# Sums of weight blocks in two channel mixers: by adding DMA transfers instead of adds on VectorE and GpSimd

## The chip, the cores and the metric

The kernel runs on one core of a Trainium2 chip. The metric is the device time of one execution in microseconds (us), from three timed executions of the kernel before. The trace that is read below is one further, profiled execution.

## The reference

The program is a two-layer backbone over 512 latent and 256 context tokens of width 1024: attention, then a SwiGLU channel mixer, in both layers. The change touches only the input projection of the channel mixers. What they compute, in float32:

```python
D_MODEL = 1024
D_FF = -(-8 * D_MODEL // (3 * 256)) * 256      # 2816

def swiglu(h, w_in, w_out):
    g, u = jnp.split(h @ w_in, 2, axis=-1)
    return (jax.nn.silu(g) * u) @ w_out

# per layer l; the context stream is updated only in layer 0
x = x + g_f * swiglu(modulate(rms_norm(x, norm_ffn_g[l]), sh_f, sc_f), ffn_w_in[l], ffn_w_out[l])
```

## The kernel before

**Precision.** TensorE multiplies a 32-bit format of lower precision, so each matrix is split into a high part (a cast on ACT, line 193) and a low part (the matrix less its high part, on VectorE or GpSimd, line 195), and each product is three matmuls (`mm3`, lines 206 to 208): high by high, high by low, low by high. `split_w` makes the pair `wh`, `wl` of a weight tile.

**One block of the mixer.** The 2816 gate columns and the 2816 up columns are taken in `FT` = 22 blocks of 128. Block j of `w_in` is a 2 by 2 matrix of tiles: A11 and A12 are the gate columns by the lower and the upper half of the model dimension, A21 and A22 the up columns. The tokens are two halves too (384 tokens each in layer 0, 256 each in layer 1), so B is also 2 by 2. Instead of eight products of tiles, the kernel makes seven (Winograd's form of Strassen's scheme), from these sums of weights: S1 = A21 + A22, S2 = S1 - A11, S3 = A11 - A21, S4 = A12 - S2. The sums of B (T1 to T4) are made once per mixer in `wino_h`. Each tile of A is 128 partitions by 512 float32, 256 KB.

**Where the weights are made.** `forms` is a generator of seven steps for one block, one per product: 11, 12, S2, S3, S1, 22, S4. Step 1 loads A11 and A12 through SyncE's queue (`load_raw`, line 184) and splits A11; step 2 splits A12; step 3 loads A21 and A22, makes S3 (line 1141), S1 (line 1142, in place of A21) and S2 (line 1143, in place of A11), and splits S2; steps 4 to 6 split S3, S1 and A22; step 7 makes S4 (line 1152, in place of A12) and splits it. `FA_ADD` and `F_ADD` say which engine adds: in layer 0 GpSimd (p) makes all four, in layer 1 VectorE (v) makes S3 and S1 and GpSimd makes S2 and S4.

**Order of the work.** `stream` strings the steps of all blocks together: two steps of blocks 0 and 1, then their five others, then all seven of each further block. `up` consumes products, and before each one `use` draws steps from the stream until 5 (layer 0) or 6 (layer 1) more are made than used. The first five steps are drawn earlier, during the second half of the attention's output projection (`ahead`). `up` then combines the seven products of a block on VectorE (lines 1198 to 1229) into gate and up tiles, and `out` multiplies them and splits the result (lines 1193 to 1196; GpSimd in layer 0, VectorE in layer 1). `down` multiplies finished blocks by the output weights in chunks of three or four blocks, interleaved with the products of the next chunk. In layer 0, VectorE also computes the next layer's modulation vectors beside the mixer (`mod_mac`, lines 392 and 394), from weights that are loaded into the same ring of buffers.

**Buffers.** Raw weights of every kind in the mixer share one ring of 10 tiles in layer 0 and 8 in layer 1 (tag `wr`); the pairs `wh`, `wl` have 5 and 6; S3 has 2 tiles of its own (tag `ws`, `NWS`). Each engine and each DMA queue works in order, and a tile framework puts in the waits. The order on each engine comes from its scheduler.

Of the kernel before, what the change touches and what calls it, by code (L numbers as in the profile page):

```python
# [10 lines left out]
F32 = mybir.dt.float32  # L11
# [3 lines left out]
ALU = mybir.AluOpType  # L15
# [3 lines left out]
P = 128  # L19
# [7 lines left out]
SPREAD0, SPREAD1 = 3, 4  # L27
AHEAD = 2
STATS_AT = 1
FA_ADD = ("pppp", "vvpp")  # L30
F_ADD = ("pppp", "vvpp")
F_LO = ("vvvvvvv", "vvvvvvv")
MACS = (0, 4, 5, 1, 6, 7, 2, 8, 9, 3, 10, 11)
MAC_LAG = 3
# [10 lines left out]
NWS = 2  # L45
# [51 lines left out]
def f32(ap):  # L97
    return ap.bitcast(F32)


class Kernel:
# [1022 lines left out]
    def forms(self, layer, j, f):  # L1124


        fa, lo = (F_ADD if j >= AHEAD else FA_ADD)[layer], F_LO[layer]

        def raw(i, h):
            return self.load_raw(self.I["w_in"][layer, j, i][:, h:h + 512], 512)  # L1130

        def split(i, name, a):
            f[name] = self.split_w(a, 512, lo_by=lo[i])
        a11, a12 = raw(0, 0), raw(0, 512)
        split(0, "11", a11)
        yield
        split(1, "12", a12)
        yield
        a21, a22 = raw(1, 0), raw(1, 512)
        s3 = self.wp.tile([P, 512], F32, tag="ws", name=self.nm("ws"), bufs=NWS)  # L1140
        self.by(fa[0]).tensor_sub(s3, a11, a21)
        self.by(fa[1]).tensor_add(a21, a21, a22)
        self.by(fa[2]).tensor_sub(a11, a21, a11)  # L1143
        split(2, "S2", a11)
        yield
        split(3, "S3", s3)
        yield
        split(4, "S1", a21)
        yield
        split(5, "22", a22)  # L1150
        yield
        self.by(fa[3]).tensor_sub(a12, a12, a11)
        split(6, "S4", a12)
        yield

# [15 lines left out]
    def up(self, layer, j, B, n, z, stream, together):  # L1171


        nc = self.nc
        v = nc.vector
        f = self.f[j]

        def use(count=1):
            self.used += count
            while self.ready < self.used + LOOK[layer]:  # L1180
                if next(stream, 0) == 0:
                    break

        def prod(a, b):
            use()
            ps = self.psM()[:, :n]
            for k in range(4):
                ws = slice(k * P, (k + 1) * P)
                self.mm3(ps, (f[a][0][:, ws], f[a][1][:, ws]), B[b][k], k == 0, k == 3)
            return ps  # L1190

        def out(g, u, half):
            self.by(Z_MUL[layer][half]).tensor_mul(g, g, u)
            zh, zl = (t[:, half * n:half * n + n] for t in z[j])
            nc.scalar.copy(zh, g)
            self.by(Z_LO[layer][half]).tensor_sub(zl, g, f32(zh))
        p, c11 = self.c_tile(n), self.c_tile(n)
        nc.scalar.copy(p, prod("11", "11"))
        yield
        v.tensor_add(c11, p, prod("12", "21"))  # L1200
        yield
        five = (("S2", "T2"), ("S3", "T3"), ("S1", "T1"), ("22", "T4"), ("S4", "22"))
        if together:

            use(5)
            ps = [self.psM()[:, :n] for _ in five]
            for k in range(4):
                ws = slice(k * P, (k + 1) * P)
                for i in (4, 2, 1, 0, 3):
                    x, y = five[i]  # L1210
                    self.mm3(ps[i], (f[x][0][:, ws], f[x][1][:, ws]), B[y][k], k == 0, k == 3)
            ps = iter(ps)
        else:
            ps = (prod(*x) for x in five)
        v.tensor_add(p, p, next(ps))
        nc.scalar.activation(c11, c11, AF.Silu)
        yield
        u3, c22 = self.c_tile(n), self.c_tile(n)
        v.tensor_add(u3, p, next(ps))
        yield  # L1220
        q = next(ps)
        v.tensor_add(c22, u3, q)
        v.tensor_add(p, p, q)
        yield
        v.tensor_add(u3, u3, next(ps))
        z[j] = self.new_z()
        out(c11, u3, 0)
        yield
        v.tensor_add(p, p, next(ps))
        self.last_silu = nc.scalar.activation(p, p, AF.Silu)  # L1230
        out(p, c22, 1)
        yield
# [709 lines left out]
```

## Time and profile before

| | us |
|---|---|
| three timed runs | 1801.03, 1806.44, 1806.47 |
| their median | 1806.44 |
| the profiled execution | 1802.62 |
| its span, first to last instruction | 1800.8 |

| engine | busy us | share of the span |
|---|---|---|
| TensorE matmul (PE) | 1698.3 | 94% |
| VectorE (DVE) | 1425.6 | 79% |
| ACT | 926.0 | 51% |
| GpSimd (POOL) | 509.0 | 28% |

In the span, layer 0's mixer is prepared from about 440 us and runs to about 1050 us; layer 1's is prepared from about 1405 us and runs to the end. TensorE's mean granted clock is 0.974 of full speed. The DMA queues moved 186.21 MB, 103 GB/s over the span, of which GpSimd's software queue moved 8.49 MB, all of it outside the mixers. Matmuls overlap, so the duration of one is longer than the time between two.

### The profile page before, as it was taken

How to read it: one execution, taken by the hardware profiler on the slowest of the kernel's cores; microseconds unless marked ns; L12 is line 12 of the kernel's file. 1: busy time of each engine (PE TensorE's matmuls, PEld its weight loads, DVE VectorE, ACT ScalarE, POOL GpSimd, SP SyncE). 2: the span in 40 equal slices, each digit the busy share in tenths (PEclk: the TensorE clock that was granted, in tenths of full speed). 3: DMA queues.
4: the chain of work that ended last, by engine and by line, in shares of the span. 5: the costliest groups of instructions: out<-in, count | busy, mean ns of one | idle time of the engine just before them, and what ended most of it. 6: DMA issues, size and time to landing. Idle time of an engine off the chain costs nothing. (4 is left out here: it accounts for less than half of the span.)

```text
span 1800.8 us, 30907 instructions
## 1 busy us (share of the span) xinstructions
PE 1698.3 (94%) x11032; PEld 1592.9 (88%) x11032; DVE 1425.6 (79%) x3060; ACT 926.0 (51%) x2222; POOL 509.0 (28%) x586
## 2 busy tenths in 40 slices
PE   6899999999898999999999989999999879999999
PEld 5789888999778999999989988999998869999997
DVE  4788877566788888888888677888788689888886
ACT  5566668655553333333323466776676555444442
POOL 1400002211674443444443252222221342111110
PEclk9999999999889999999999999999999989999999
DMA  9533233234113434344334313111123423333332
GB/s 315 172 113 116 81 99 99 62 115 158 33 41 108 130 111 133 110 122 128 104 111 141 97 44 105 48 53 48 48 71 110 139 63 106 106 106 100 106 100 83
DMA packets 125754, 186.21 MB, mean 103 GB/s; under 512 B 10625, under 2 KB 63504, under 8 KB 125600
## 3 DMA queue, kind: packets, MB, share of 16 engines
q1 hardware_dynamic: 119360, 172.53, 31.1%
q0 software_dynamic: 2496, 8.49, 1.5%
q10 hardware_dynamic: 3744, 3.23, 0.6%
q8 instruction: 87, 1.43, 0.3%
q14 instruction: 67, 0.55, 0.1%
HBM read 174.70 MB, written 13.70 MB: 105 GB/s over the span
## 5 line engine op out<-in xcount | busy, mean ns | idle before, releaser
L193 ACT CAST wh<-wr 128x512 fp32r<-128x512 f32 (+4 forms) x465 | 287.7, 624 | 385.8 <-PE psM L207 232.3
L195 DVE TENSOR_TENSOR wl<-wr,wh 128x512 fp32r<-128x512 f32 (+3 forms) x433 | 353.2, 819 | 49.0 <-ACT wh L193 42.9
L208 PE MATMUL psD<-zh,wl 128*128 128x384 f32 (+1 forms) x512 | 185.4, 362 | 16.7 <-DVE wl L195 16.7
L206 PE MATMUL psD<-zh,wh 128*128 128x384 f32 (+1 forms) x512 | 184.0, 359 | 6.4 <-ACT wh L193 6.4
L711 PE MATMUL psW<-wh,hh 128*128 128x384 f32 (+2 forms) x543 | 183.4, 339 | 3.9 <-ACT wh L193 3.2
L207 PE MATMUL psD<-zl,wh 128*128 128x384 f32 (+1 forms) x512 | 183.4, 358 | 0.0
L712 PE MATMUL psW<-wl,hh 128*128 128x384 f32 (+2 forms) x543 | 181.2, 334 | 0.0
L713 PE MATMUL psW<-wh,hl 128*128 128x384 f32 (+2 forms) x543 | 179.8, 332 | 0.0
L207 PE MATMUL psM<-bl,wh 128*128 128x256 f32 x616 | 174.8, 284 | 3.9 <-POOL bl L467 3.6
L206 PE MATMUL psM<-bh,wh 128*128 128x256 f32 x616 | 173.8, 284 | 4.8 <-ACT bh L466 2.7
L208 PE MATMUL psM<-bh,wl 128*128 128x256 f32 x616 | 172.7, 281 | 0.0
L207 PE MATMUL psM<-hl,wh 128*128 128x384 f32 (+1 forms) x416 | 139.4, 335 | 3.2 <-POOL hl L467 2.8
L206 PE MATMUL psM<-hh,wh 128*128 128x384 f32 (+1 forms) x416 | 139.8, 337 | 2.6 <-ACT hh L466 1.8
L195 POOL TENSOR_TENSOR wl<-wr,wh 128x512 fp32r<-128x512 f32 (+2 forms) x32 | 39.8, 1248 | 352.4 <-ACT wh L193 330.4
L1143 POOL TENSOR_TENSOR wr<-wr,wr 128x512 f32<-128x512 f32 x44 | 60.8, 1383 | 273.9 <-DVE wl L195 225.4
L208 PE MATMUL psM<-hh,wl 128*128 128x384 f32 (+1 forms) x416 | 137.9, 331 | 0.0
L394 DVE SCALAR_TENSOR_TENSOR wr<-wr,silc,wr 128x512 f32<-128x512 f32 x112 | 105.4, 950 | 27.1 <-DMA wr<-in_mod_w 26.7
L207 PEld LDWEIGHTS psM<-bl,wh 128*128 128x128 f32 x616 | 118.1, 192 | 8.5 <-POOL bl L467 6.1
L206 PEld LDWEIGHTS psM<-bh,wh 128*128 128x128 f32 x616 | 117.7, 192 | 8.1 <-ACT bh L466 3.8
L208 PEld LDWEIGHTS psD<-zh,wl 128*128 128x128 f32 x512 | 96.8, 189 | 30.8 <-DVE wl L195 23.3
L1371 POOL TENSOR_TENSOR nbm<-nb,namask 128x128 f32<-128x128 f32 x144 | 64.7, 466 | 200.4 <-DVE nam L1399 180.0
L208 PEld LDWEIGHTS psM<-bh,wl 128*128 128x128 f32 x616 | 117.9, 191 | 0.0
(414 smaller groups left out, 4789.4 us busy)
## 6 DMA issues: line engine op xcount, KB each, us to landing
wr<-in_w_in SPq DMA_DIRECT2D x176, 256.0 KB, 2.9
wr<-in_mod_w SPq DMA_DIRECT2D x96, 256.0 KB, 2.7
mraw<-in_mod_w SPq DMA_DIRECT2D x32, 512.0 KB, 4.0
wr<-in_w_dn SPq DMA_DIRECT2D x50, 256.0 KB, 2.7
wr<-in_w_na SPq DMA_DIRECT2D x28, 384.0 KB, 3.2
wr<-in_w_out SPq DMA_DIRECT2D x36, 256.0 KB, 2.7
wr<-in_w_dn SPq DMA_DIRECT2D x48, 192.0 KB, 2.4
modw<-in_mod_w SPq DMA_DIRECT2D x8, 1024.0 KB, 9.6
```

The source lines that it names most:

```text
L193: nc.scalar.copy(hi[:, :n], raw[:, :n])
L195: (nc.gpsimd if on_pool else nc.vector).tensor_sub(lo[:, :n], raw[:, :n], f32(hi[:, :n]))
L206: t.matmul(out, w[0], x[0], start=first, stop=False)
L207: t.matmul(out, w[0], x[1], start=False, stop=False)
L208: t.matmul(out, w[1], x[0], start=False, stop=last)
L394: v.scalar_tensor_tensor(acc[cd], raw, self.sc[:, k, cd:cd + 1], acc[cd], ALU.mult, ALU.add)
L711: nc.tensor.matmul(ps, hh[:, ts], hi[:, o:o + n], start=k == 0, stop=False)
L712: nc.tensor.matmul(ps, hh[:, ts], lo[:, o:o + n], start=False, stop=False)
L713: nc.tensor.matmul(ps, hl[:, ts], hi[:, o:o + n], start=False, stop=k == KD - 1)
L1143: self.by(fa[2]).tensor_sub(a11, a21, a11)
L1371: nc.gpsimd.tensor_tensor(o, bj[:, t0 + t], m, ALU.add)
```

## The change

All four sums of a block are made by DMA transfers that add what they read to what stands at their destination (`accum_op=ALU.add`), issued from GpSimd's queue. Such a transfer can only add, so the signs are turned: the block is treated as if A11 and A12 were negated. With S1 = A21 + A22 as before, S2 = A11 + S1, S3' = A11 + A21 and S4' = A12 + S2. The products of 11, S3' and S4' then come with the other sign, and three combinations on VectorE in `up` become subtractions of the same shape.

A21 gets A22 added straight from device memory; a second copy of A11 is loaded into S3's tile, and A21 is added to it from device memory; the finished S1 tile is added to A11's tile, and the finished S2 tile to A12's tile, both from one place in SBUF to another. The loads of A21 and A22 move from step 3 to step 2, ahead of the split of A12. The four adds on VectorE or GpSimd of each block go. Per block that is one more plain load of 256 KB on SyncE's queue and four adding transfers of 256 KB on GpSimd's; there are 44 blocks in the two layers.

```diff
-FA_ADD = ("pppp", "vvpp")
-F_ADD = ("pppp", "vvpp")
@@ forms
-        fa, lo = (F_ADD if j >= AHEAD else FA_ADD)[layer], F_LO[layer]
+        lo = F_LO[layer]
+
+        def src(i, h):
+            return self.I["w_in"][layer, j, i][:, h:h + 512]
 
         def raw(i, h):
-            return self.load_raw(self.I["w_in"][layer, j, i][:, h:h + 512], 512)
+            return self.load_raw(src(i, h), 512)
+
+        def add(t, x):
+            self.nc.gpsimd.dma_start(t, x, accum_op=ALU.add)
 
         def split(i, name, a):
             f[name] = self.split_w(a, 512, lo_by=lo[i])
-        a11, a12 = raw(0, 0), raw(0, 512)
+        a11, a12 = (t[:, :512] for t in (raw(0, 0), raw(0, 512)))
         split(0, "11", a11)
         yield
+        a21, a22 = (t[:, :512] for t in (raw(1, 0), raw(1, 512)))
+        s3 = self.wp.tile([P, 512], F32, tag="ws", name=self.nm("ws"), bufs=NWS)
+        nc = self.nc
+        nc.sync.dma_start(s3, src(0, 0))
+        add(a21, src(1, 512))
+        add(s3, src(1, 0))
         split(1, "12", a12)
         yield
-        a21, a22 = raw(1, 0), raw(1, 512)
-        s3 = self.wp.tile([P, 512], F32, tag="ws", name=self.nm("ws"), bufs=NWS)
-        self.by(fa[0]).tensor_sub(s3, a11, a21)
-        self.by(fa[1]).tensor_add(a21, a21, a22)
-        self.by(fa[2]).tensor_sub(a11, a21, a11)
+        add(a11, a21)
         split(2, "S2", a11)
         yield
         split(3, "S3", s3)
         yield
+        add(a12, a11)
         split(4, "S1", a21)
         yield
         split(5, "22", a22)
         yield
-        self.by(fa[3]).tensor_sub(a12, a12, a11)
         split(6, "S4", a12)
         yield
@@ up
-        v.tensor_add(p, p, next(ps))
+        v.tensor_sub(p, next(ps), p)
...
-        v.tensor_add(u3, p, next(ps))
+        v.tensor_sub(u3, p, next(ps))
...
-        v.tensor_add(p, p, next(ps))
+        v.tensor_sub(p, next(ps), p)
```

## Rows read from the trace of the kernel before

**Rows 1.** Stretches: start:end us, length, busy us (x instructions), clock, DMA share, GB/s.
```profile
440.00:520.00 80.00, 67.11 (x289) 57.15 (x288) 64.33 (x117) 46.28 (x103) 51.38 (x41) 0.81 0.19 64
600.00:700.00 100.00, 95.70 (x549) 94.21 (x548) 86.98 (x146) 32.65 (x62) 42.10 (x34) 1.00 0.38 117
...
1415.00:1420.00 5.00, 2.12 (x14) 1.83 (x12) 1.64 (x5) 3.11 (x7) 0.00 (x0) 0.81 0.81 302
1440.00:1470.00 30.00, 19.98 (x102) 15.85 (x102) 25.55 (x48) 18.37 (x43) 16.63 (x19) 0.84 0.15 48
1600.00:1700.00 100.00, 100.00 (x710) 92.80 (x708) 87.00 (x160) 49.13 (x93) 15.53 (x12) 1.00 0.35 104
```

**Rows 2.** Waits of TensorE, 440 to 1050 us: total us, times, longest us.
```profile
PE psD L208 <- DVE wl L195: 15.1, 10, 3.9
PE psD L206 <- ACT wh L193: 6.4, 1, 6.4
...
PE psM L208 <- POOL wl L195: 2.6, 1, 2.6
```

**Rows 3.** Timeline of VectorE in layer 1's mixer: start us, us, engine line operation.
```profile
1606.11 0.68 DVE L195 TENSOR_TENSOR wl<-wr,wh 128x512 fp32r<-128x512 f32 x1
...
1611.64 1.21 DVE L195 TENSOR_TENSOR wl<-wr,wh 128x512 fp32r<-128x512 f32 x1 [0.17 <-ACT wh L193]
```

**Rows 4.** Groups of VectorE, 565 to 1045 us: busy us, mean ns | idle before.
```profile
L195 DVE TENSOR_TENSOR wl<-wr,wh 128x512 fp32r<-128x512 f32 x116 | 96.2, 830 | 11.6 <-ACT wh L193 11.3
L394 DVE SCALAR_TENSOR_TENSOR wr<-wr,silc,wr 128x512 f32<-128x512 f32 x100 | 91.8, 926 | 27.1 <-DMA wr<-in_mod_w 26.7
```

**Rows 5.** Groups of GpSimd, 565 to 1045 us: the four adds.
```profile
L1143 POOL TENSOR_TENSOR wr<-wr,wr 128x512 f32<-128x512 f32 x18 | 26.0, 1447 | 39.3 <-DVE wl L195 24.6 <-DMA wr<-in_mod_w 10.1 <-issue 4.3
L1141 POOL TENSOR_TENSOR ws<-wr,wr 128x512 f32<-128x512 f32 x17 | 24.2, 1426 | 91.7 <-DMA wr<-in_w_in 87.0 <-DVE wl L195 4.7
L1142 POOL TENSOR_TENSOR wr<-wr,wr 128x512 f32<-128x512 f32 x17 | 23.8, 1398 | 9.0 <-DMA wr<-in_w_in 5.8 <-DVE x L1098 1.3 <-DVE wl L195 1.2
L1152 POOL TENSOR_TENSOR wr<-wr,wr 128x512 f32<-128x512 f32 x18 | 23.6, 1311 | 47.8 <-DVE wl L195 32.6 <-issue 12.6 <-DMA wr<-in_mod_w 2.7
```

**Rows 6.** Groups of the whole span by shape: VectorE's adds in layer 1.
```profile
L1141 DVE TENSOR_TENSOR ws<-wr,wr 128x512 f32<-128x512 f32 x22 | 17.0, 773 | 1.5 <-DMA wr<-in_w_in 1.4
...
L1142 DVE TENSOR_TENSOR wr<-wr,wr 128x512 f32<-128x512 f32 x22 | 15.1, 684 | 0.7 <-DMA wr<-in_w_in 0.6
```

**Rows 7.** GpSimd's DMA issues in the attention of layer 1: ns min/median/max.
```profile
L1364 POOL DMA_DIRECT2D nb<-rpb_exp x16: 546/563/622, 1070.3 to 1327.7; - x16
```

**Rows 8.** The page's DMA issues: count, KB each, median us to landing.
```profile
mraw<-in_mod_w SPq DMA_DIRECT2D x32, 512.0 KB, 4.0
...
nb<-rpb_exp POOLq DMA_DIRECT2D x16, 256.0 KB, 2.9
```

**Rows 9.** The 176 loads of mixer weights, 256 KB each: time to landing.
```profile
DMA to landing us min/median/max: 2.4/2.9/7.2
```

**Rows 10.** Timeline of GpSimd in layer 1's mixer: S2's adds of two blocks.
```profile
1611.01 1.29 POOL L1143 TENSOR_TENSOR wr<-wr,wr 128x512 f32<-128x512 f32 x1 [12.02 <-DVE wl L195]
...
1626.31 1.30 POOL L1143 TENSOR_TENSOR wr<-wr,wr 128x512 f32<-128x512 f32 x1 [12.04 <-DVE wl L195]
```

**Rows 11.** Timeline of ACT in layer 1's mixer: casts after that of A12.
```profile
1613.66 0.62 ACT L193 CAST wh<-wr 128x512 fp32r<-128x512 f32 x1 [2.05 <-PE psD L207]
...
1616.46 0.62 ACT L193 CAST wh<-wr 128x512 fp32r<-128x512 f32 x1 [0.69 <-PE psM L207]
```

**Rows 12.** Waits of ACT, 1515 to 1740 us: total us, times, longest.
```profile
ACT wh L193 <- PE psM L207: 58.2, 83, 0.9
```

**Rows 13.** The chain that ended last, in order of time: start us, us, what.
```profile
1409.37 6.75 DMA wr<-in_w_in
...
1506.20 1.63 POOL wr L1143
```

**Rows 14.** Waits of VectorE, 600 to 1000 us: total us, times, longest.
```profile
DVE wr L394 <- DMA wr<-in_mod_w: 25.5, 30, 1.6
```

## Prediction

> **What bounds the kernel now.** I read the page first (TensorE busy for 94% of the span), then the table of stretches, then the waits of TensorE inside the mixers, then the timelines of the engines that feed it, and last the chain that ended last. The table shows two kinds of stretch [rows 1]. Inside the mixers TensorE is the bound: 95.70 of 100 us in layer 0 and 100.00 of 100 us in layer 1, at full clock. On the way into a mixer it is not: 67.11 of 80 us from 440 us on, at a clock of 0.81, and 19.98 of 30 us from 1440 us on, at 0.84. So in the steady part of layer 1 nothing that feeds TensorE can gain; the gain can only come from layer 0's steady part and from the two ways in. What TensorE waits for in layer 0 is the low parts of weights from VectorE, 15.1 us in ten waits, one wait of 6.4 us for a cast, and one of 2.6 us for a low part that GpSimd makes, which stands behind adds on GpSimd's queue [rows 2]. VectorE is busy for 87 of 100 us in both layers [rows 1], so small delays on it reach TensorE.
>
> **What the change removes.** In layer 0, four adds per block on GpSimd, 1447 + 1426 + 1398 + 1311 ns = 5.6 us per block, 97.6 us between 565 and 1045 us [rows 5]. GpSimd has slack, so its own time is worth nothing but for the queue. What they cost is VectorE's time: the same subtraction of 128 by 512 takes 0.68 us when GpSimd rests and 1.21 us while GpSimd makes S2 and S4 [rows 3, 10]. In layer 0 the mean is 830 ns over 116 [rows 4], so 116 x 0.15 = 17 us are such waiting; at the same 18% another 17 us of L394's 91.8. The adds are 97.6 of 480 us, 20 in 100, against GpSimd's 42.10 in 100 altogether [rows 1], so about half of those 34 us goes, 17 us of VectorE in 480.
>
> The Trainium skill (SBUF — State Buffer, Who interferes with whom) says that a VectorE instruction with two SBUF inputs contends with a GpSimd instruction that reads SBUF, by a lock that is held for the whole instruction. The trace's 0.68 against 1.21 us agrees.
>
> In layer 1, two adds per block on VectorE, 773 + 684 ns, together 32.1 us [rows 6], and two on GpSimd. TensorE waits for neither in the steady part, so they are worth nothing there.
>
> **What it adds.** Per block four issues on GpSimd, by the only issues there that the trace has at 0.563 us each [rows 7], so 2.3 us, against 5.6 us of adds before; it is less than before even at twice that. One more load on SyncE, hidden as long as the ring has room.
>
> The unknown is L, the time from the issue of an adding transfer of 256 KB to its landing; the trace has none. From below: 2.9 us, a plain transfer of that size from the same queue [rows 8]. From above: 7.2 us, the slowest load of that size among loads that queue behind each other [rows 9]. An adding transfer reads both addends, 512 KB, and a plain load of 512 KB takes 4.0 us [rows 8]. I take 4 us, and keep both ends.
>
> The Trainium skill (Collectives: The Full Stack, The bandwidth ceiling) says that an adding transfer costs twice a copy because it issues two reads, and that the addition itself costs nothing. No row here shows it; by it L would be near my 4 us.
>
> **Where that time lies.** In layer 1 a block takes 1626.31 - 1611.01 = 15.3 us [rows 10]. The add into A11 may start when the low part of A11 is done, at 1611.0, and the cast of S2 is one of those at 1613.66 to 1616.46 [rows 10, 11]: 2.7 to 5.5 us for L. If L is longer, ACT waits for the rest, and behind it in its order the casts of S3, S1 and of the output weights. But casts run ahead: ACT waits for TensorE to free `wh`, 83 times [rows 12], and with six pairs and some ten casts in 15.3 us the lead is 6 x 1.53 = 9 us, less 1.3 us for cast (0.62) and low part (0.68): 7 to 8 us [rows 3, 11]. So S2 reaches TensorE late only if L is above 10 us or so.
>
> The tighter loop is GpSimd's own queue. The add into A11 waits for the sum in A21 to land, the add into A12 waits for the sum in A11 to land, and the next block's first add stands behind it: two landings and two issues that are not covered, 2 L + 1.1 us plus some hand-over, about 2 L + 2 per block. At L = 4 that is 10 of 15.3 us; it binds from L = 6.6 on. Queued behind a waiting issue in layer 0 are the multiplications of gate and up tiles, and behind those ACT's casts of them; the adds of before stood there too and waited for the same low parts, so at L = 4 the extra is some 3 us per block, and finished blocks are needed a chunk later.
>
> **The transfers.** In layer 1 the engines are busy for 0.35 at 104 GB/s [rows 1], so full is 297 GB/s, 4.5 MB in 15.3 us, of which 1.6 are used. Added are 0.26 MB for the load and 4 x 0.52 MB if both reads count: 3.9 MB, 87%. If the writes count as much, 5.0 MB, 110%. Layer 0 has a like share (0.38) and longer blocks.
>
> **The ways in.** At layer 1's, the chain that ended last runs for 6.75 us through a load of mixer weights, while the transfers move 302 GB/s at 0.81 [rows 1, 13]: every transfer that now stands ahead costs 0.87 us (262 KB at 302 GB/s). Block 1's A11 and A12 now queue behind block 0's A21, A22 and S3, 2.6 us, and share with up to four adding transfers, 4 x 1.7 = 7 us more. What ACT does behind those casts (the squares of the norm) is on the chain. Ends 0 and +9.5 us for each way in; I take +1.5 each, since only casts of block 1 are late.
>
> **The sum.** Layer 0's waits for low parts: half of 15.1, -7.5 us (ends 0 and -21.5, with the 6.4 us). GpSimd's low part behind adds: half of 2.6, -1.3 us (ends 0, -2.6). On the chain in layer 1 the S2 add of 1.63 us [rows 13] goes for a landing that was issued earlier: -1 us (ends -1.6, and +2.4 if it takes 4 us in its place). The ways in: +3 us (ends 0, +19). Layer 1's steady part: 0. Together -6.8 us. The profiled execution took 1802.62 us, its span 1800.8; the three runs shown have a mean of 1804.6 and a median of 1806.44. Less 6.8 from the mean: 1798 us. About 0.3% is what a measurement here can tell from no change, 5.4 us.
>
> **The rivals.**
>
> (1) *Slower: the transfers become layer 1's bound.* Either GpSimd's loop, from L = 6.6 on, or the engines themselves, from 4.5 MB per block on. At L = 8 a block takes 18 us, +2.7, for some 20 blocks +54 us; at 110% a block takes 16.8 us, +31 us. Center +30 us, 1835. For: 87% of the engines by the milder count, bursts, and loads that already take up to 7.2 us. Against: 2.9 us from the same queue, and a loop that has 5 of 15.3 us to spare at L = 4. It would show as ACT waiting for a DMA at the cast of S2.
>
> (2) *Slower: the ways in.* The burst falls where TensorE is already idle and at a low clock, and the norm's work on GpSimd stands behind issues that wait for landings. +6 to +19 us, center +12, 1817. For: the chain runs through a load there. Against: of block 0, whose products come first, A11 and A12 are loaded before all that is added, and GpSimd's queue is rid of adds of 1.4 us each.
>
> (3) *No change: the relief is spent on the modulation weights.* VectorE waited 30 times, 25.5 us, for those loads [rows 14]. The mixer's tiles now stand longer in the same ring of 10 (A21 and A22 a step, A11 one landing), so these loads start later and share the engines. If each of the hundred such loads is 0.2 us later, the 17 us are gone: 1805. The same holds if an issue holds VectorE off as an add did, so that the change doesn't relieve what it should.
>
> **How the numbers follow.** Forecast 0.42, rival (1) 0.20, (2) 0.15, (3) 0.20, others 0.03. The likeliest is 1798, with its own range 1789 to 1806. Faster by over 0.3%: 0.85 of the forecast and 0.2 of (3), 0.40. Within: 0.13 of the forecast, 0.6 of (3), a little of the rest, 0.23. Slower: 0.37. Cases of both signs are near each other in weight. The range: down to 1786 (most of the 21.5 us), up to 1835, where half of (1) is left out.
>
> **What would show it.** Right: adding transfers land in under 5 us; VectorE's L195 in layer 0 falls from 830 towards 750 ns; TensorE's waits for `wl` in layer 0 fall to about 8 us; layer 1 keeps 100 of 100 us busy. Wrong: TensorE below 97 of 100 us at 1600 us with ACT waiting for a DMA (rival 1); the start of layer 1's steady part later against the end of the attention by over 5 us (rival 2); L394's waits above 40 us (rival 3).

## The result, and the profile after

The changed kernel takes 1867.3 us, the median of four runs (1856.3 to 1868.5), against 1805.9 (1801.0 to 1806.5) for the kernel before beside it: a ratio of 1.033, 95% interval 1.031 to 1.035, some 60 us slower. The forecast was 1798 with a range up to 1835. It was wrong in sign, and the time lies outside the range.

The lines shown here stand two numbers lower in the changed kernel than in the kernel before (L193 there is L195 before, L191 is L193, L392 is L394, L204 to L206 are L206 to L208, L182 is L184). The adding transfers are all issued at L1134, and the load into S3's tile at L1144.

The stretches of [rows 1] in the changed kernel (start:end, length, busy us of TensorE, its weight loads, VectorE, ACT, GpSimd, then clock, DMA share, GB/s):

```profile
440.00:520.00 80.00, 62.67 (x277) 53.23 (x276) 63.55 (x115) 45.19 (x101) 42.13 (x40) 0.84 0.38 98
600.00:700.00 100.00, 91.58 (x514) 89.46 (x512) 73.58 (x138) 30.71 (x58) 31.54 (x31) 0.98 0.63 159
700.00:800.00 100.00, 92.16 (x513) 91.20 (x514) 68.52 (x132) 30.30 (x56) 30.93 (x31) 0.95 0.63 161
1440.00:1470.00 30.00, 22.68 (x149) 21.79 (x148) 21.36 (x51) 19.11 (x46) 15.53 (x18) 0.79 0.79 182
1600.00:1700.00 100.00, 94.46 (x643) 85.06 (x643) 66.22 (x129) 41.81 (x82) 20.18 (x23) 0.98 0.70 171
```

In layer 1 TensorE fell from 100.00 to 94.46 of 100 us, in layer 0 from 95.70 to 91.58, and the granted clock is no longer 1.00 in either (0.95 to 0.98). VectorE is busy for 73.58 instead of 86.98 us in layer 0, a part of it because less work gets done in the stretch (138 instructions instead of 146). The stretch that [rows 1] lacks, in the kernel before:

```profile
700.00:800.00 100.00, 97.99 (x566) 96.70 (x565) 85.87 (x148) 32.29 (x60) 42.19 (x33) 1.00 0.40 120
```

No engine is at its limit any more, so the time went into waits. TensorE's own in layer 0, 440 to 1050 us (total us, times, longest), against [rows 2]:

```profile
PE psD L206 <- DVE wl L193: 32.8, 16, 5.7
PE psM L205 <- POOL hl L465: 7.7, 6, 4.2
...
PE psD L204 <- ACT wh L191: 3.2, 1, 3.2
```

The wait for low parts doubled, from 15.1 to 32.8 us. What VectorE did there, 565 to 1045 us, by groups (busy us, mean ns | idle before), against [rows 4], and its wait from 600 to 1000 us, against [rows 14]:

```profile
L193 DVE TENSOR_TENSOR wl<-wr,wh 128x512 fp32r<-128x512 f32 x115 | 89.6, 779 | 18.4 <-ACT wh L191 18.3
L392 DVE SCALAR_TENSOR_TENSOR wr<-wr,silc,wr 128x512 f32<-128x512 f32 x100 | 79.1, 800 | 63.9 <-DMA wr<-in_mod_w 63.6
```

```profile
DVE wr L392 <- DMA wr<-in_mod_w: 58.4, 35, 4.4
```

Each low part is 51 ns shorter and each modulation step 126 ns: 115 x 0.051 + 100 x 0.126 = 18.5 us saved in these two groups. But the wait for modulation weights grew from 25.5 to 58.4 us, which is more than was saved, and the low parts stand behind it in VectorE's order.

The DMA issues on the page of the changed kernel (count, KB, median us to landing), against [rows 8, 9], then the modulation weights in the kernel before, then GpSimd's issues in the changed kernel (ns min/median/max), against [rows 7]:

```profile
wr<-in_w_in SPq DMA_DIRECT2D x176, 256.0 KB, 3.4
wr<-in_mod_w SPq DMA_DIRECT2D x96, 256.0 KB, 3.2
wr<-wr POOLq DMA_DIRECT2D x88, 256.0 KB, 3.7
...
wr<-in_w_in POOLq DMA_DIRECT2D x44, 256.0 KB, 5.1
ws<-in_w_in POOLq DMA_DIRECT2D x44, 256.0 KB, 5.7
```

```profile
wr<-in_mod_w SPq DMA_DIRECT2D x96, 256.0 KB, 2.7
```

```profile
L1134 POOL DMA_DIRECT2D wr<-wr x88: 865/874/1241, 463.5 to 1819.8; - x88
L1134 POOL DMA_DIRECT2D wr<-in_w_in x44: 863/882/1064, 444.5 to 1808.4; - x44
```

In layer 1 the place is seen in ACT's waits, 1515 to 1740 us, against [rows 12]; before, the casts of weights waited there for TensorE and for no transfer:

```profile
ACT wh L191 <- DMA wr<-wr: 59.0, 14, 7.4
...
ACT wh L191 <- PE psM L205: 32.0, 42, 6.2
```

And how it comes about, in three timelines of one block of layer 1 (GpSimd, SyncE's queue, ACT; start us, us, engine line operation, idle before), against the 15.3 us of [rows 10]:

```profile
1645.58 0.88 POOL L1134 DMA_DIRECT2D wr<-wr  x1 [3.68 <-issue]
1652.28 0.88 POOL L1134 DMA_DIRECT2D wr<-in_w_in  x1 [5.82 <-DMA wr<-in_w_in]
...
1657.88 0.87 POOL L1134 DMA_DIRECT2D wr<-wr  x1 [2.80 <-DVE wl L193]
1662.60 0.87 POOL L1134 DMA_DIRECT2D wr<-wr  x1 [3.85 <-DVE c L1229]
```

```profile
1649.03 0.80 SPq L182 DMA_DIRECT2D wr<-in_w_in  x2
```

```profile
1662.14 0.62 ACT L191 CAST wh<-wr 128x512 fp32r<-128x512 f32 x1 [1.32 <-DMA wr<-wr]
```

Read it as a ring of waits. At 1645.58 GpSimd issues the addition into A12. When it has landed, 3.3 us later, A11's tile, from which it read, is free and SyncE can load the next A21 and A22 (1649.03). A21 lands 3.1 us later, and A22 is added to it from memory (1652.28). That sum lands 5.1 us later and is added to A11 (1657.88). That lands 4.2 us later; S2 is cast at once (1662.14), and the next addition into A12 goes (1662.60). The steps are 3.45 + 3.25 + 5.60 + 4.72 = 17.0 us, a ring of four landings; a block on TensorE takes 15.3. The block shown is one of the shorter ones: from the addition into A12 at 1559.29 us to the one fifteen blocks on, at 1819.80, the mean is 17.4 us. (The profile names the releaser that came last. At 1657.88 that is the low part of A11, which ended at 1657.47, within 0.1 us of the landing; at 1662.60 it is a step of VectorE that runs from 1662.10 to 1662.51, while S2's sum had landed at 1662.1: again both, within half a us.)

### The profile page after: what moved, and what is told of

Read it like the earlier page. It is cut to its first block, busy times and chain, and to the rows that moved or that the text cites. A ratio compares the mean times of both kernels' runs of the same rounds, so it can differ in the third digit from the quotient of the medians.

```text
span 1865.2 us, 31278 instructions
## 1 busy us (share of the span) xinstructions
PE 1720.7 (92%) x11032; PEld 1608.0 (86%) x11032; DVE 1347.7 (72%) x3016; ACT 919.9 (49%) x2222; POOL 477.0 (26%) x630
## 3 DMA queue, kind: packets, MB, share of 16 engines
q0 software_dynamic: 27840, 54.63, 16.7%
## 5 line engine op out<-in xcount | busy, mean ns | idle before, releaser
L191 ACT CAST wh<-wr 128x512 fp32r<-128x512 f32 (+4 forms) x465 | 285.9, 623 | 421.0 <-PE psM L205 197.5
L193 DVE TENSOR_TENSOR wl<-wr,wh 128x512 fp32r<-128x512 f32 (+3 forms) x433 | 320.2, 745 | 120.2 <-ACT wh L191 117.0
L206 PE MATMUL psD<-zh,wl 128*128 128x384 f32 (+1 forms) x512 | 192.1, 375 | 42.8 <-DVE wl L193 42.8
L204 PE MATMUL psD<-zh,wh 128*128 128x384 f32 (+1 forms) x512 | 189.0, 369 | 16.9 <-ACT wh L191 15.3
L205 PE MATMUL psD<-zl,wh 128*128 128x384 f32 (+1 forms) x512 | 187.7, 367 | 0.3 <-DVE zl L1202 0.3
L204 PE MATMUL psM<-bh,wh 128*128 128x256 f32 x616 | 175.3, 286 | 6.7 <-ACT wh L191 4.1
L206 PE MATMUL psM<-bh,wl 128*128 128x256 f32 x616 | 174.5, 284 | 0.2 <-DVE wl L193 0.2
L1134 POOL DMA_DIRECT2D wr<-wr x88 | 77.9, 889 | 337.2 <-DVE wl L193 130.5
L206 PEld LDWEIGHTS psD<-zh,wl 128*128 128x128 f32 x512 | 99.6, 195 | 63.5 <-DVE wl L193 55.9
L204 PE MATMUL psM<-hh,wh 128*128 128x384 f32 (+1 forms) x416 | 141.3, 340 | 2.3 <-ACT hh L464 1.2
L206 PE MATMUL psM<-hh,wl 128*128 128x384 f32 (+1 forms) x416 | 139.6, 335 | 0.0
L392 DVE SCALAR_TENSOR_TENSOR wr<-wr,silc,wr 128x512 f32<-128x512 f32 x112 | 90.3, 816 | 65.0 <-DMA wr<-in_mod_w 64.7
L193 POOL TENSOR_TENSOR wl<-wr,wh 128x512 fp32r<-128x512 f32 (+2 forms) x32 | 39.2, 1238 | 350.6 <-ACT wh L191 332.0
L204 PEld LDWEIGHTS psM<-bh,wh 128*128 128x128 f32 x616 | 119.9, 195 | 10.3 <-ACT wh L191 5.6
L204 PEld LDWEIGHTS psD<-zh,wh 128*128 128x128 f32 x512 | 99.0, 193 | 27.0 <-ACT wh L191 19.1
L206 PEld LDWEIGHTS psM<-bh,wl 128*128 128x128 f32 x616 | 119.5, 194 | 0.7 <-DVE wl L193 0.7
```

What stands on the lines that cost most here:

```text
L191: nc.scalar.copy(hi[:, :n], raw[:, :n])
L193: (nc.gpsimd if on_pool else nc.vector).tensor_sub(lo[:, :n], raw[:, :n], f32(hi[:, :n]))
L204: t.matmul(out, w[0], x[0], start=first, stop=False)
L205: t.matmul(out, w[0], x[1], start=False, stop=False)
L206: t.matmul(out, w[1], x[0], start=False, stop=last)
L392: v.scalar_tensor_tensor(acc[cd], raw, self.sc[:, k, cd:cd + 1], acc[cd], ALU.mult, ALU.add)
```

## The experiments

My theory after the result was that ring for layer 1, and for layer 0 the late modulation weights. The rivals were throughput of the transfers (their engines were busy for 0.70 of the time), GpSimd's order by itself, and, in layer 0, tiles held longer because A21 and A22 are loaded a step earlier. Ratios are to the kernel before run on the same chip beside them.

### Which layer loses

Both kernels take `forms` and the signs of the change in one layer and those of before in the other.

```diff
+DMA_SUMS = (True, False)       # e_layer1_only: (False, True)
...
+    def forms(self, layer, j, f):
+        return (self.forms_dma if DMA_SUMS[layer] else self.forms_eng)(layer, j, f)
```

> The block sums come by adding transfers in layer 0's channel mixer alone; layer 1's is as before. From the two profiles, layer 0's mixer ended 24 us later and layer 1 lost the rest of 64. If each layer's loss is its own: about +24 us (1830). If layer 1's loss is what the late start of its loads leaves behind (a loss handed on from layer 0): +50 or more. If layer 0's loss is a drift of the clock that only comes with the whole change: under +10.

> The adding transfers in layer 1's channel mixer alone. If each layer's loss is its own: about +38 us (1844), +2 of it on the way in and +36 in the steady part, where a block takes 17.0 us instead of 15.3. The forecast's step (layer 1 steady part unchanged, ways in +3) would give +3 (1809).

Measured: 1823.3 us, ratio 1.0085 (1.0056 to 1.0113), and 1850.6 us, 1.0245 (1.0219 to 1.0272): 15 and 44 us. They add up to 59 of some 60, so each layer's loss is its own. Layer 0's had been read as 24 us from one pair of profiles. In five profiles with layer 0 as before, the attention behind it starts at 1073.4 to 1084.4 us; in six with layer 0 as in the change it starts at 1089.4 to 1097.4, and the two means differ by 17 us.

### Layer 1: room, order, landings

Three edits of the changed kernel: more raw tiles; GpSimd's order; both.

```diff
-RAW0, RAW1, WR0, WR1 = 10, 8, 5, 6
+RAW0, RAW1, WR0, WR1 = 10, 12, 5, 6     # e_ring12; 14 in e_ring14 and e_ring14_order
```

```diff
-        add(a21, src(1, 512))     # e_order, e_ring14_order
-        add(s3, src(1, 0))
+        if layer in (1,) and j >= AHEAD:
+            with self.tc.issue_after(self.last_sum.ins):
+                add(a21, src(1, 512))
+                add(s3, src(1, 0))
...
-        add(a12, a11)
+        self.last_sum = add(a12, a11)
```

> The changed kernel with 12 raw tiles in layer 1 instead of 8. Theory of the held tiles: A11's tile comes free only when the addition into A12 has landed, the next block's A21 and A22 wait for that tile, their addition waits for them, and so on around: three landings in a loop of 17.0 us. With twelve tiles the next block's loads no longer wait, and layer 1's +36 us goes: 1830. Rival, transfers' bandwidth (more traffic makes each load late): stays at 1867. Rival, the GpSimd queue in order (issues of 0.87 us and waits one behind the other): stays at 1860 to 1867, with the wait of SyncE gone and ScalarE's wait for the adding transfers still at 53 us.

Measured: 1875.7 us, 1.039 (1.035 to 1.043). The expectation that more room alone opens the ring failed. SyncE still waited 145.2 us for adding transfers between 1550 and 1790 us, where it had waited 131.4 in the change. The order of the instructions on GpSimd showed why: the scheduler had put the next block's transfers from memory, which wait for that block's loads, ahead of this block's sums:

```profile
1613.82 1.18 POOL L1134 DMA_DIRECT2D wr<-in_w_in  x1
1614.54 1.36 POOL L1134 DMA_DIRECT2D wr<-wr  x1
1621.43 0.88 POOL L1134 DMA_DIRECT2D wr<-wr  x1 [5.53 <-issue]
```

The addition at 1614.54 can't belong to the block of the transfer at 1613.82, whose sum had not landed. So room only moved the ring by a block: the additions into A12 follow each other at 18.2 us in the mean of 14 blocks. That led to the next three.

> The changed kernel with 14 raw tiles in layer 1 instead of 8, and there each block's two adding transfers from memory put behind the addition into A12 of the block before, in GpSimd's queue (so far they stood ahead of it, and waited for their own loads). With twelve tiles alone SyncE still waited 145 us for the adding transfers between tiles, since the next block's loads, the transfers from memory and the sums of the block before stand in one ring of waits of 17.5 to 18 us. This kernel opens it: a block's loads wait for a block two before it, and GpSimd's own round is about 1.8 (two issues) + 5 + 0.9 + 3.7 + 0.9 = 12 us, below the 15.3 of TensorE. Theory of the ring of waits: layer 1's loss of 36 us goes nearly whole, 1827 to 1838, and what is left is layer 0's 24. Rival, bandwidth (the engines of the transfers are 70% busy, and each load is late for that): 1860 to 1876. Rival, GpSimd's queue alone: about 1867, with GpSimd still waiting for loads.

> The changed kernel with its 8 raw tiles in layer 1 and only GpSimd's order mended (a block's two transfers from memory behind the addition into A12 of the block before). With fourteen tiles and this order layer 1's loss fell from 44 to 9 us. Theory of the ring of waits: with eight tiles the next block's A22 still waits for the addition into A12 and the ring of load (3.9), transfer from memory (5.4), and two landings (3.4 each) with their issues stays at about 17 us: 1855 to 1870. If GpSimd's order alone was the cause: 1825 to 1835.

> The changed kernel with 14 raw tiles in layer 1 and GpSimd's order left as the change has it. Order alone gave 1867, fourteen tiles with the order 1831. Theory of the ring of waits: the order ties the sums of a block behind the next block's loads, so the room alone opens nothing: 1855 to 1880. If the room alone is what counts: 1825 to 1840.

Measured: both edits 1830.6 us, 1.0132 (1.0113 to 1.0152); the order alone 1866.8, 1.0347 (1.0319 to 1.0374); the room alone 1871.1, 1.0366 (1.0339 to 1.0394). Neither edit gains anything alone, and together they take away 36 us, to 24 over before, of which layer 0's share is 15. In the change with its 8 tiles GpSimd's order is mostly the mended one already (1645.58, then 1652.28 above), so the order alone had little to move; it is with more room that the scheduler turns it round. Both results fit the ring, and neither GpSimd's order alone nor the room alone explains the loss. Some 9 us of layer 1's 44 are left, most of them at the start of the mixer (TensorE is busy there for 26.21 of 30 us from 1530 us on); their cause was not tested. In the profile of the kernel with both (a stretch as above, the median landing from 1520 to 1780 us, GpSimd's timeline):

```profile
1600.00:1700.00 100.00, 100.00 (x709) 92.90 (x708) 75.44 (x147) 48.39 (x94) 22.53 (x26) 1.00 0.79 190
```

```profile
wr<-in_w_in SPq DMA_DIRECT2D x61, 256.0 KB, 4.6
```

```profile
1644.75 0.87 POOL L1134 DMA_DIRECT2D wr<-wr  x1 [3.37 <-DVE wl L193]
1645.30 1.23 POOL L1134 DMA_DIRECT2D wr<-in_w_in  x1
...
1660.31 0.87 POOL L1134 DMA_DIRECT2D wr<-wr  x1 [3.63 <-issue]
```

TensorE is back at 100.00 of 100 us, and a block takes 1660.31 - 1644.75 = 15.6 us, though the transfers now carry 190 GB/s with their engines busy for 0.79, more than the 171 and 0.70 of the change. Plain loads land as late as 4.6 us there, and the tiles cover it. So in this stretch the bytes are not the limit.

The other way to open the ring is to shorten it: two of its landings become additions on GpSimd, in both layers.

```diff
-        add(a11, a21)
+        nc.gpsimd.tensor_add(a11, a11, a21)
...
-        add(a12, a11)
+        nc.gpsimd.tensor_add(a12, a12, a11)
```

> The changed kernel, but the two sums between tiles (S2 and S4) are made by GpSimd's own additions, in both layers; only S1 and S3 come by adding transfers from memory. An addition takes 1.26 us where a transfer took 0.88 to issue and 3.7 to land, so a block's ring of waits is shorter by two landings (about 6 us). Theory of the ring of waits: layer 1's 36 us goes nearly whole, while layer 0's loss is smaller or the same: 1815 to 1835. Rival, bandwidth: half of the adding transfers are gone (the load of the transfers falls from 70% to some 55%), and the loss with it: about 1840 to 1850.

Measured: 1825.6 us, 1.0106 (1.0078 to 1.0134). TensorE is at 100.00 of 100 us from 1600 us on, with the ring of 8 tiles and without a mended order. Layer 1's loss is gone (from the last bias of the attention to the end the profile has 435.5 us, before 437.8); what is left is layer 0's.

### Is it the traffic?

The kernel before, with the change's traffic in layer 1 added for nobody. The first version let the scheduler place the transfers:

```diff
+            nc.gpsimd.dma_start(a, w[1][:, 512:1024], accum_op=ALU.add)
+            nc.gpsimd.dma_start(b, w[1][:, 0:512], accum_op=ALU.add)
+            nc.sync.dma_start(tr[4], w[0][:, 0:512])
...
+            self.nc.gpsimd.dma_start(self.tr[5], self.tr[2 - 2 * (j % 2)], accum_op=ALU.add)
...
+            self.nc.gpsimd.dma_start(self.tr[5], self.tr[3 - 2 * (j % 2)], accum_op=ALU.add)
```

> The kernel before, to which layer 1's channel mixer gets the change's traffic with nobody waiting for it: per block one more 256 KB load on SyncE, two adding transfers from memory and two between tiles issued by GpSimd, into scratch tiles. The sums are still made by the engines. Theory of the held tiles: within 8 us of before (1806 to 1814; what remains is load latency). Rival, bandwidth: most of the +36 us of layer 1 (1835 to 1845). Rival, the GpSimd issues (4 x 0.87 us a block beside its own work): +5 to +20.

Measured: 1906.5 us, 1.056 (1.053 to 1.059). It tests nothing. The transfers ran ahead of their blocks, two of them wrote one tile, and GpSimd, in order, stood still for them with the blocks' sums behind (1500 to 1800 us):

```profile
POOL tr L1162 <- DMA tr<-tr: 66.0, 14, 6.9
```

The second version ties a block's traffic behind its last sum and last load, and gives each transfer its own tile; the third has a ninth raw tile.

```diff
+            with self.tc.issue_after(self.last_load.ins):
+                nc.sync.dma_start(tr[4], self.I["w_in"][layer, j, 0][:, 0:512])
+            with self.tc.issue_after(last.ins):
+                for t, x in ((0, w[1][:, 512:1024]), (1, w[1][:, 0:512]), (2, tr[5]), (3, tr[5])):
+                    nc.gpsimd.dma_start(tr[t], x, accum_op=ALU.add)
```

> As the earlier kernel with the traffic alone, whose adding transfers ran ahead of the blocks they were meant for and held up GpSimd, so that it tested nothing: now the four adding transfers of a block and its further load are tied behind the block's last sum and last load, write four tiles of their own, and nobody waits for them within a block. The engines make the sums, as before. Rival, bandwidth: most of layer 1's 36 us is there, 1835 to 1845. Theory of the ring of waits: 1806 to 1814, with the transfers' share of 70% in layer 1 and PE at 100 of 100. Rival, issues on GpSimd (4 x 0.87 us a block): +2 to +10, with ScalarE's wait for L1159's sum.

> The kernel with the traffic alone (1844, 38 us over before; its VectorE waited 46 us for the blocks' own loads, whose landing had gone from 2.9 to 4.7 us), with nine raw tiles in layer 1 instead of eight, so that each load can start one tile earlier, some 2.5 us. If the traffic costs by the later landing of loads that are asked for just in time: the loss falls below 15 us (1806 to 1820). If it costs as throughput of the transfers' engines, which the tile doesn't change: 1838 to 1846. A value between says that 2.5 us cover only part of the lateness.

Measured: 1843.9 us, 1.020 (1.018 to 1.022), which is what the rival, bandwidth, foretold and not what my theory did; with one more tile 1826.1 us, 1.0129 (1.0106 to 1.0152). Waits of VectorE from 1550 to 1790 us, and the median landing from 1520 to 1780 us, of the second version (L1148 and L1147 are lines 1142 and 1141 of the kernel before, S1 and S3):

```profile
DVE wr L1148 <- DMA wr<-in_w_in: 23.1, 13, 3.2
DVE ws L1147 <- DMA wr<-in_w_in: 22.6, 14, 4.4
```

```profile
wr<-in_w_in SPq DMA_DIRECT2D x62, 256.0 KB, 4.7
```

The same in the kernel before:

```profile
DVE ws L1141 <- DMA wr<-in_w_in: 1.4, 1, 1.4
DVE wr L1142 <- DMA wr<-in_w_in: 0.6, 1, 0.6
```

```profile
wr<-in_w_in SPq DMA_DIRECT2D x58, 256.0 KB, 2.9
```

So the traffic does cost time when nobody waits for it: plain loads land 1.8 us later, and the kernel before asks for A21 and A22 just in time. It costs as lateness at least in part, since one tile of lead takes away 13 of 36 us with the same bytes. With that tile, TensorE is held up in one stretch and not in the next:

```profile
1600.00:1700.00 100.00, 95.85 (x663) 88.05 (x663) 83.21 (x149) 44.37 (x87) 37.46 (x36) 0.98 0.73 180
1700.00:1750.00 50.00, 49.98 (x358) 46.13 (x357) 39.69 (x72) 23.03 (x45) 18.21 (x18) 1.00 0.76 184
```

Whether the other 23 us would go with still more tiles wasn't tried, so throughput isn't excluded for them. For the change itself the answer is in the kernel with room and order.

### Layer 0

> The kernel before with one thing of the change alone: A21 and A22 are loaded one step earlier, at the step of A12's form, so that each block holds two raw tiles longer. The sums are made as before. If layer 0's 24 us come from the raw tiles held longer by the earlier loads (SyncE then gives the modulation weights and the down weights later): about +15 to +24 there (1821 to 1830). If they come from the adding transfers' landings (a tile is held until what reads it has landed): 0 to +5 (1806 to 1811).

```diff
+        a21, a22 = raw(1, 0), raw(1, 512)
         split(1, "12", a12)
         yield
-        a21, a22 = raw(1, 0), raw(1, 512)
```

Measured: 1803.1 us, 0.9979 (0.9963 to 0.9996). The earlier loads cost nothing; if anything they help.

The next pair leaves out the modulation of layer 1, in the kernel before and in the changed one.

```diff
-        mac = macs()
+        mac = iter(())
+        nc.vector.memset(self.modT[:, 1], 0.5)
```

> The kernel before without the modulation of layer 1: its 96 loads and their VectorE steps in layer 0's channel mixer are left out and the modulation is set to 0.5 (a part of the computation is left out). It is the base for the kernel beside it, and should be some 10 to 25 us below before, since TensorE's waits for low parts in layer 0 (15 us) go with VectorE's load: 1780 to 1797.

> The changed kernel without the modulation of layer 1 (the same part left out). Layer 0 loses about 15 us by the change (the kernel with it in layer 0 alone), layer 1 about 44. Theory of the late modulation weights (with the adding transfers SyncE gets to their loads later and they land later; VectorE, in order, waits 60 us for them in layer 0 instead of 26, and the low parts behind it are late): layer 0's loss goes, and the kernel is 40 to 48 us above the one beside it. Rival, GpSimd in order (the products of the gate stand behind adding transfers that wait; ScalarE waits for them as before the loads were left out): 56 to 65 us above it.

Measured: 1781.2 and 1822.6 us, 0.9861 (0.9837 to 0.9884) and 1.0093 (1.0065 to 1.0121). The change costs 41 us without the modulation and 60 with it: what remains is layer 1's, and layer 0's loss is gone but for some 4 us (the attention behind it starts at 1050.0 us, and at 1045.6 in the kernel beside it). In layer 0 of the changed one no wait of TensorE for a low part of the mixer is left; one wait for a cast, of 10.1 us, is. This shows that layer 0 loses by way of the modulation. It does not tell late loads from VectorE's want of slack, since the edit takes both away. The wait of 58.4 us above speaks for the loads.

Which part of the change makes them late? The kernel below keeps the transfers between tiles (S2, S4) and gives S1 and S3 back to the engines; it is the mirror of the one with S2 and S4 on GpSimd.

```diff
-        nc.sync.dma_start(s3, src(0, 0))
-        add(a21, src(1, 512))
-        add(s3, src(1, 0))
+        by = (nc.gpsimd, nc.vector)[layer]
+        by.tensor_add(s3, a11, a21)
+        by.tensor_add(a21, a21, a22)
```

> The changed kernel, but S1 and S3 are made by the engines (GpSimd in layer 0, VectorE in layer 1) from tiles that are loaded one step earlier; S2 and S4 still come by the two adding transfers between tiles, and A11 is not loaded a second time. Theory of the ring of waits: a ring of load, sum, landing, landing is left in layer 1, shorter by the landing of the transfer from memory (5 to 6 us) and longer by VectorE's sum behind its queue: layer 1's loss falls to 5 to 20 us; with layer 0's 5 to 15, 1816 to 1840. Rival, bandwidth (the adding transfers' bytes are down by half, two reads and a load less): 1830 to 1840.

Measured: 1815.0 us, 1.0053 (1.0037 to 1.0069). In layer 1 TensorE is at 96.22 of 100 us from 1600 us on, and the additions into A12 follow each other at 16.3 us in the mean of 15 blocks (1523.30 to 1767.68): a shorter ring still binds, as was expected, though the time is 1 us below the 1816 to 1840 given. In layer 0 the two mirrors differ. Waits from 600 to 1000 us, S1 and S3 by transfers from memory, then S2 and S4 by transfers between tiles:

```profile
DVE wr L392 <- DMA wr<-in_mod_w: 47.6, 31, 4.2
PE psD L206 <- DVE wl L193: 30.5, 13, 6.3
```

```profile
DVE wr L392 <- DMA wr<-in_mod_w: 30.6, 33, 2.0
PE psD L206 <- DVE wl L193: 7.5, 6, 2.5
```

TensorE's wait in the kernel before, then in the kernel with the early loads alone:

```profile
PE psD L208 <- DVE wl L195: 13.9, 9, 3.9
```

```profile
PE psD L208 <- DVE wl L195: 11.4, 7, 3.9
```

VectorE's wait is 25.5 us before [rows 14]. So the transfers from memory, with their third load, double both waits or nearly so. With the transfers between tiles TensorE's wait is about half of before, as the forecast said of the whole change; 2.5 of the 6.4 us come with the early loads, which this kernel has too (one profile of each). Tiles held by the transfers between tiles are not what costs layer 0: SyncE waits for those 35.1 us from 580 to 1040 us in this kernel, which loses nothing there (the attention behind it starts at 1067.0 us), and 41.8 in the change. The last pair has the better half in layer 0 alone; the second of them also loads A21 and A22 earlier in layer 1.

```diff
+DMA_SUMS = (True, False)       # layer 0: the edit above; layer 1: as before
```

> In layer 0 the sums between tiles (S2, S4) come by adding transfers and S1, S3 from GpSimd, with A21 and A22 loaded one step earlier; layer 1 is the kernel before. In the profile of the kernel with S1 and S3 made by the engines, layer 0 ended 6 us earlier than before and VectorE waited 34 us for modulation weights, while with S1 and S3 by transfers from memory (and S2, S4 by engines) it ended 27 us later with 56 us of such waits. If it is the reads from memory, with the third load, that cost layer 0, and the transfers between tiles give the relief that was forecast: 3 to 7 us below before (1798 to 1802). If the 6 us are the spread of profiles: 1803 to 1808.

> As the kernel beside it, and layer 1 too loads A21 and A22 one step earlier (its sums by the engines, as before). The kernel with the early loads in both layers alone was 3 us below before. If that gain was layer 1's and adds up: 1796 to 1800; if it was layer 0's (which has it here anyway) or spread: as the kernel beside it, within 2 us.

Measured: 1796.4 us, 0.9941 (0.9920 to 0.9963), and 1797.2 us, 0.9941 (0.9918 to 0.9964). Both are faster than the kernel before, by 11 us with intervals that stay below 1, and they beat the change by 70. The early loads of layer 1 add nothing. The second of them differs from the kernel with the early loads alone by layer 0's transfers between tiles, and by S1 and S3 being added a step earlier there: 0.9941 against 0.9979, some 7 us for the relief. It is weakly shown, since the two intervals touch (0.9964 and 0.9963) and the two were run on different chips.

## Why the prediction was wrong, step by step

- **What bounds the kernel** was read rightly: layer 1's steady part could gain nothing, and layer 0 hung on low parts.
- **The relief of VectorE** was right in kind and size: 17 us were forecast and 18.5 came, though shared otherwise: 5.9 on the low parts and 12.6 on the modulation, where about half and half was forecast. L195's mean in layer 0 was to go from 830 towards 750 ns; it is 779.
- **L** was taken as 4 us for all four. It is 3.7 us from tile to tile and 5.1 and 5.7 us from memory. "Under 5 us" holds for one half of them.
- **The issues** show 0.87 us each instead of 0.563, but where GpSimd waits for nothing they follow each other at 0.55 us (1644.75, 1645.30); they cost nothing that the runs show.
- **"Layer 1's steady part: 0"** is the term that failed, by way of the loop that it rests on: GpSimd's queue at 2 L + 2 = 10 us per block, "it binds from L = 6.6 on". That loop was sized rightly, as 5.60 + 4.72 = 10.3 us, but it is not closed there. A21 can't be loaded until the addition into A12 has landed and freed A11's tile (3.45), nor added to until it has landed itself (3.25). With those two steps the ring is 17.0 us in the block shown and 17.4 in the mean, against 15.3, and it binds though the landings' medians, 3.7 to 5.7 us, are all below 6.6. The condition that would have led there, "as long as the ring has room", stands in the prediction, but for the one further load alone (which goes to S3's own tiles), and the room was never worked out. Rival (1) had the sign of it (TensorE below 97 of 100 us, ACT waiting for a DMA at the cast of S2: both came) and a chance of 0.20, at +30 us; it is +44.
- **The transfers at 87% or 110%** as rival (1)'s other cause: not what binds the change's steady part, with TensorE at 100.00 of 100 us at a share of 0.79 once the ring is open. That an adding transfer costs its engines about two transfers is borne out: GpSimd's queue took 16.7 - 1.5 = 15.2% of the engines' time for 54.63 - 8.49 = 46.14 MB, 1.9 times as long per byte as SyncE's 172.53 MB in 31.1% of the span before (spans of 1865.2 and 1800.8 us). The Trainium skill (Collectives: The Full Stack, The bandwidth ceiling) says of the add in a reduce-scatter that it needs two source reads and so pushes twice the traffic of a copy; the 1.9 agrees.
- **The slack of S2's cast**, 7 to 8 us of lead, can't help against such a ring: a lead covers a late start once, not 1.7 to 2.1 us in each block.
- **Layer 0's waits for low parts**, -7.5 us, is the second term that failed: they came out at +17.7 (32.8 against 15.1). Rival (3) named the mechanism (L394's waits above 40 us; they are 58.4) and mis-sized it: it let the relief be just eaten. Landing grew by 0.5 us for each modulation load (2.7 to 3.2), besides their later issue, and the loss was 15 us. That the modulation is the way is shown by the pair without it; that it is the lateness of its loads, and not VectorE's want of slack beside them, is argued from the waits. In the mixed kernel, without the adding reads from memory, TensorE's waits fall to about half (7.4 us from 600 to 1000 us), and its time is 1796: the forecast's mechanism, with the early loads' share in it, in a kernel that does half of the change in one layer.
- **The ways in**, +3 us together: layer 1's is 3.1 us longer (the first output of its `down` stands 147.0 us behind the last bias of the attention, 143.9 before: 1534.8 - 1387.8 and 1506.9 - 1363.0). Layer 0's is no longer: the first output of its `down` stands at 558.2 us, before at 560.6. So the sum came out small, as forecast, but not as 1.5 each; one pair of profiles says no more.
- **The two small terms**: the wait for GpSimd's low part, 2.6 us, is gone from layer 0 (forecast: half of it); the one of -1 us on layer 1's chain was not read apart.
- **The range** ended at 1835, which is rival (1) at +30 us with no relief, so with rival (3) as it was priced. Both happened, in different layers, and both were priced too low: 44 us for 30, and a loss of 15 for none.

## What to carry over

A transfer that combines tiles holds its source and its target until it has landed, and whoever reloads them waits as long. Before handing sums to such transfers, write the ring of tile reuse out, landing by landing, and compare its sum with the time of a block; here it took either two landings less, or both tiles for a second block and an order on the issuing queue in which no transfer waits ahead of the sums that free those tiles. Transfers from tile to tile may relieve a crowded engine; those that read memory again make other loads late, and what is loaded just in time pays.

## What the runs showed of the hardware

An adding transfer of 256 KB landed in a median of 3.7 us from tile to tile and in 5.1 and 5.7 us from memory, where plain loads of that size took 3.4 in the same kernel, and it took 1.9 times the transfer engines' time per byte. Added traffic, at an engine share of 0.71 from 1600 us on, lengthened the landing of plain 256 KB loads from 2.9 to 4.7 us; with the ring open, plain loads landed in 4.6 us at a share of 0.79 and 190 GB/s, and TensorE ran at 100.00 of 100 us. Four adding transfers issued one behind the other landed late: those from tile to tile took 9.2 us in the traffic kernel from 1520 to 1780 us, against 3.4 in the change. Waits in TensorE's stream can come with a lower granted clock: from 600 and from 700 us on it is 1.00 before, and 0.98 and 0.95 in the changed kernel, whose longest wait for a low part is 5.7 us. They need not: with layer 1 alone changed, the clock stays at 1.00 where TensorE is busy for 91.15 of 100 us:

```profile
1600.00:1700.00 100.00, 91.15 (x635) 82.50 (x633) 63.28 (x123) 40.89 (x81) 20.57 (x24) 1.00 0.72 171
```
